# Layer 0 of an encoder kernel: eight output blocks over each x tile at the start, one first transfer, 25 warming products

## The chip, the cores and the metric

The kernel runs on one core of a Trainium2 chip. The metric is the device time of one execution in microseconds (us). Five engines matter: TensorE (PE, products), VectorE (DVE), ScalarE (ACT), GpSimd (POOL) and SyncE (SP, which issues most transfers).

## The reference

A trunk of two layers over 256 tokens and 1024 channels, float32, one batch. In each layer a normalised x goes through one large input projection; three mixers (a gated short convolution, a pooling mixer and windowed attention with grouped heads) are gated and added, and a SwiGLU follows:

```
h = rms_norm(x, g_mix)
proj = h @ w_in
b_a, c_a, x_a, u_p, q, k, v, ga, gp, gt = jnp.split(proj, split_points(), axis=-1)
y_a = short_conv_mixer(b_a, c_a, x_a, conv_w, w_a_out)
y_p = multiscale_pool_mixer(u_p, w_pool, pool_scale)
y_t = windowed_gqa(q, k, v, rel_bias, sink) @ w_attn_out
x = x + (sigmoid(ga) * y_a + sigmoid(gp) * y_p + sigmoid(gt) * y_t) @ w_o
gate, up = jnp.split(rms_norm(x, g_ffn) @ w_gu, [D_FF], axis=-1)
return x + (jax.nn.silu(gate) * up) @ w_down
```

## The kernel before

x lies transposed in SBUF: 128 channels on the partitions, eight x tiles (k = 0 to 7) of 256 tokens. Every matrix is cut into blocks of 128 x 128. All blocks lie in memory in the order in which they are used, which `plan_layer` writes out; 16 blocks make a chunk of 1 MB (`raw`), eight make a half chunk. A block's product is three matmuls of the float32r format (`mm3`, L161 to L165): the weights are split into `hi` and `lo` (`convert`, L136 on ACT and L137 on DVE), the activations likewise, and PE does hi x h (L163), hi x lo part of x (L164) and lo x h (L165). Below, "product" is one such matmul; a half chunk is 24 products.

`advance` keeps the conversions three half chunks ahead of PE. There are three `raw` buffers and five of `hi` and of `lo`, so a chunk's transfer waits until the third chunk before it is converted, and a conversion waits until PE is done with the fifth half chunk before it. The first two chunks arrive in pieces, with the x tiles between them (`dma_chunk`, L116 to L127), all issued by SP; the channel vectors `ch` (g_mix, g_ffn, the convolution's taps and the pooling scale) come first.

Normalisation is split. The first projections use `xg`, x times g_mix without the row factor (`xg_tiles`, L242: a pair h, lo for each x tile, h by DVE for the first two x tiles and by ACT after them, lo by DVE). Meanwhile `squares` sums the squares, `norm_stats` (L280) sums them over the partitions on PE (L283) and makes the reciprocal root `rr` through ACT (L285, then a table load) and a chain of small DVE steps, and `norm_rows` (L294) spreads it over the rows as `r` by four products (L299). What used `xg` is multiplied by `r` later. `make_h` makes the fully normalised pairs `h` for the later projections; it is issued after gate block MH.

Layer 0 starts with 21 products on a tile of zeros (`warm`, WARM = 21, L181). Then come K and V over each x tile in turn (`quad_outer`: four output blocks per x tile, 12 products), then the eight Q blocks one by one over all x tiles (`ntile`), with the sums (L283) after the first Q block, the rows (L299) and `kv_out` after the second, and the transposes of V (`vp`, L459) after the fourth. Eight gate blocks follow, then the convolution's blocks, with the attention's steps between them. PSUM has two pools of four banks, psA and psB.

A tile framework orders the instructions: a scheduler places the code's instructions on each engine's queue, and `issue_after` keeps a group behind one instruction. Each engine works through its queue in order.

Of the kernel before, what the change touches and what calls it, by code (L numbers as in the profile page):

```python
# [25 lines left out]
CB, CC, CX, CU, CQ, CK, CV, CGA, CGP, CGT = 0, 8, 16, 24, 32, 40, 42, 44, 52, 60  # L26
CT = 16
# [5 lines left out]
    HEADS += [4 * (2 * _p) + _g, 4 * (2 * _p + 1) + _g]  # L33


def plan_layer(last):

    out = []

    def inner(mat, ns, nk=KT):  # L40
        for n in ns:
            for k in range(nk):
                out.append((mat, k, n))

    def outer(mat, ns, nk=KT):
        for k in range(nk):
            for n in ns:
                out.append((mat, k, n))

    outer("in", (CK, CK + 1, CV, CV + 1))  # L50
    for q in range(2):
        inner("in", [CQ + 4 * q + j for j in range(4)])
    inner("in", [CGA + n for n in range(8)])
    for n in range(8):
        inner("in", (CC + n, CX + n, CB + n))
    inner("in", (CU, CU + 1))
    inner("a", range(8))
    for n in range(8):
        inner("in", (CGP + n, CGT + n))
        if n % 2 == 1 and n < 7:  # L60
            inner("in", (CU + n + 1, CU + n + 2))
        inner("t", (n,))
        out.extend(("pool", k, n) for k in range(2))
        if n >= 2:
            out.extend(("o", n - 2, m) for m in range(8))
    for j in range(4):
        out.extend(("o", k, m) for k in (6, 7) for m in (2 * j, 2 * j + 1))
    for q in range(NQ):
# [16 lines left out]


NCH = len(plan_layer(False)) * L // CT


@with_exitstack  # L90
def trunk(ctx, tc, wst, xT, chp, sinkb, rb, invc, gfin, ident_d, out):
    nc = tc.nc
    V, S, G, PE = nc.vector, nc.scalar, nc.gpsimd, nc.tensor

    const = ctx.enter_context(tc.tile_pool(name="const", bufs=1))
# [13 lines left out]

    plan = []  # L110
    for l in range(L):
        plan += [(l,) + key for key in plan_layer(l == L - 1)]
    raws, his, los = {}, {}, {}
    state = {"pos": 0, "dma": 0, "cv": 0}

    def dma_chunk(c):  # L116
        raw = wp.tile([P, CT * P], F32, name=f"raw{c}", tag="raw", bufs=3)
        if c < 2:
            if c == 0:
                nc.sync.dma_start(ch, chp)  # L120
            for a, b, xa, xb in (((0, 4, 0, 1), (4, 8, 1, 2), (8, 12, 2, 3), (12, 16, 3, 4)),
                                 ((0, 8, 4, 6), (8, 16, 6, 8)))[c]:
                nc.sync.dma_start(raw[:, a * P:b * P], wst[c, :, a * P:b * P])
                nc.sync.dma_start(x[:, xa:xb], xT[:, xa:xb])
# [54 lines left out]
    wps = psA.tile([P, 2 * T], F32, name="wps", tag="A")  # L179
    for _ in range(WARM):  # L180
        PE.matmul(wps[:, :T], warm[:, :P], warm, start=True, stop=True)  # L181
    x = act.tile([P, KT, T], F32, name="x")
    ch = const.tile([P, L, 6, KT], F32, name="ch")
    dma_chunk(0)
    dma_chunk(1)
    dma_chunk(2)
# [52 lines left out]
        return t[:, 0, :], t[:, 1, :]  # L239


    def xg_tiles(l, gi, j, st):  # L242

        for k in (2 * j, 2 * j + 1):
            g = ch[:, l, gi, k:k + 1]
            h, lo = pair(act, "xz", 8, "xg")
            if j < XJ:
                V.tensor_scalar(h, x[:, k], g, None, op0=ALU.mult)  # L248
            else:
                S.activation(h, x[:, k], AF.Copy, scale=g)  # L250
            V.scalar_tensor_tensor(lo, x[:, k], g, h.bitcast(F32), op0=ALU.mult, op1=ALU.subtract)  # L251
            st["xg"].append((h, lo))
# [41 lines left out]
    def norm_rows(st):  # L294

        rr, ps = st["q"], st["ps"]
        for i in range(4):
            tb = i % 2
            PE.matmul(ps[:, T:], rr[:, i:i + 1].to_broadcast([P, P]), ident2[:, P - tb * P:3 * P - tb * P],  # L299
                      start=(i == 0), stop=(i == 3))  # L300
# [21 lines left out]
    def newB(name="b"):  # L322
        return psB.tile([P, 2 * T], F32, name=nm(name), tag="B")
# [1 line left out]
    def newA(name="a"):  # L325
        return psA.tile([P, 2 * T], F32, name=nm(name), tag="A")

    def quad_outer(l, mat, ns, xs):
        banks = [newB(), newB()]
        for k in range(KT):  # L330
            for i, n in enumerate(ns):
                mm3(banks[i // 2][:, half(i % 2)], (l, mat, k, n), xs[k][0], xs[k][1],
                    start=(k == 0 and i % 2 == 0), stop=(k == KT - 1), skip=True)
        return banks

    def ntile(l, mat, n, xs, dst, nk=KT, koff=0):
        for k in range(nk):
            mm3(dst, (l, mat, k, n), xs[koff + k][0], xs[koff + k][1], start=(k == 0), stop=(k == nk - 1))
# [70 lines left out]
    def mixer(l, st):  # L409
        xg = st["xg"]  # L410
        def kv_out():
            norm_rows(st)
# [12 lines left out]
            for p in range(2):  # L425
                f = t1("vf")
                V.tensor_tensor(f[:, ::-1], vb[:, half(p)], r, op=ALU.mult)
                vf.append(f)
            return r, vf

        kb, vb = quad_outer(l, "in", (CK, CK + 1, CV, CV + 1), xg)
        ast = {"s": {}, "pt": {}, "ao": {}, "bias": {t: load_bias(t) for t in range(3)}}
        if l:
            norm_stats(st, AF.Exp)
        qs = []
        for qd in range(2):
            banks = [newB(), newB()]
            for i in range(4):
                ntile(l, "in", CQ + 4 * qd + i, xg, banks[i // 2][:, half(i % 2)])
                if l == 0 and qd == 0 and i == 0:  # L440
                    with tc.issue_after(last_mm[0].ins):
                        norm_stats(st, AF.Exp)
                if qd == 0 and i == 1 - l:
                    with tc.issue_after(last_mm[0].ins):
                        r, vf = kv_out()
# [9 lines left out]
            if qd == 0:  # L455
                for kt in range(2):
                    ps = newA("vp")
                    for p in range(2):
                        PE.transpose(ps[:, p * P:(p + 1) * P], vf[p][:, kt * P:(kt + 1) * P], ident)  # L459
                    vp = ps[:, :2 * P].rearrange("p (k j d) -> p k j d", k=2, j=2)  # L460
                    split(vt[kt][:, :, 0::3], vt[kt][:, :, 1:3], vp)
# [236 lines left out]
    st = {"xg": []}  # L698
    for j in range(4):
        convert(j)  # L700
        xg_tiles(0, 0, j, st)
    state["cv"] = 4
    for j in range(4):
        squares(j, st, V)
    with tc.issue_after(st["add"].ins):
        build_bias()
# [135 lines left out]
```

## Time and profile before

| | us |
|---|---|
| median of 3 runs | 980.25 (980.19 to 980.49) |
| the profiled execution | 981.37 |
| its span, first to last instruction | 979.6 |
| PE busy | 969.8 |
| DVE busy | 711.9 |
| ACT busy | 553.4 |

The profile is a record of one execution. Times on a timeline count from the span's start. A timeline row has the start, the duration, the engine, the line, the operation, what it writes and reads, the shape and how many instructions are merged in it; in brackets stands the idle time of the engine before it and what ended it. PE's durations overlap, so that PE's pace is read from the distance of the starts. A row of the waits has the total, the number and the longest. A row of the stretches has the stretch, its length, each engine's busy time with its instructions, the granted clock of PE, the share of time the DMA engines were busy, and GB/s.

### The profile page before, as it was taken

The numbers are of one execution on the slowest core, as the hardware profiler recorded it, in microseconds if no ns is written. First come the engines' busy times: TensorE is split into PE (matmuls) and PEld (weight loads), VectorE is DVE, ScalarE is ACT, GpSimd is POOL, SyncE is SP. The second block draws the span as 40 slices with busy tenths as digits, with TensorE's granted clock in tenths as the row PEclk, the third lists the DMA queues.
The fourth block names the chain that finished last, engine by engine and source line by source line (L and its number), as shares of the span: only waits on it lengthen the run. The fifth ranks groups of instructions, "written<-read, shape, count | busy, mean of one in ns | idle before, by whom it ended". The sixth has DMA issues, their size and how long they took to land.

```text
span 979.6 us, 19115 instructions
## 1 busy us (share of the span) xinstructions
PE 969.8 (99%) x7877; PEld 956.7 (98%) x7877; DVE 711.9 (73%) x1277; ACT 553.4 (56%) x916; POOL 41.4 (4%) x60
## 2 busy tenths in 40 slices
PE   8999999999999999999999999999999999999997
PEld 8999999999999999999999999999999999999996
DVE  7899888667668955546589888975777697555555
ACT  5866676654456544444577566765554574444443
POOL 6000000000002000000020000000000020000000
PEclk9999999999999999999999999999999999999999
DMA  8656544555554555455543745444554455545531
GB/s 299 230 192 207 184 162 160 194 177 193 183 201 171 179 181 200 179 178 195 188 173 130 248 160 181 143 170 173 185 203 173 172 194 178 209 173 188 197 132 43
DMA packets 27399, 178.11 MB, mean 182 GB/s; under 512 B 3312, under 2 KB 4096, under 8 KB 7088
## 3 DMA queue, kind: packets, MB, share of 16 engines
q1 hardware_dynamic: 25200, 169.93, 48.7%
q0 software_dynamic: 2112, 6.97, 2.5%
q8 instruction: 61, 1.00, 0.4%
q14 instruction: 26, 0.21, 0.1%
HBM read 175.80 MB, written 1.08 MB: 181 GB/s over the span
## 4 chain that ended last, share of the span: by engine, by line
PE 98%; DMA 1%; DVE 0%; ACT 0%; SPq 0%; issue 0%; DVEq 0%
PE b L164 25%; PE b L163 25%; PE b L165 25%; PE dn L165 2%; PE dn L163 2%; PE dn L164 2%; PE dn L623 2%; PE dn L622 2%; PE dn L621 2%; PE wo L163 2%; PE wo L164 2%; PE o L395 2%; PE wo L165 2%; PE pt L380 1%; PE sc L351 1%; PE sc L352 1%
## 5 line engine op out<-in xcount | busy, mean ns | idle before, releaser
L137 DVE TENSOR_TENSOR lo<-raw,hi 128x1024 fp32r<-128x1024 f32 (+1 forms) x322 | 390.0, 1219 | 208.8 <-ACT hi L136 208.3
L136 ACT ACTIVATE hi<-raw 128x1024 fp32r<-128x1024 f32 (+1 forms) x322 | 337.2, 1052 | 331.0 <-PE b L164 212.5
L163 PE MATMUL b<-h,hi 128*128 128x256 f32 x1344 | 379.8, 283 | 0.0
L165 PE MATMUL b<-h,lo 128*128 128x256 f32 x1344 | 378.4, 282 | 0.0
L164 PE MATMUL b<-h,hi 128*128 128x256 f32 x1344 | 378.3, 281 | 0.0
L164 PEld LDWEIGHTS b<-h,hi 128*128 128x128 f32 x1344 | 253.2, 188 | 0.2
L163 PEld LDWEIGHTS b<-h,hi 128*128 128x128 f32 x1344 | 253.2, 188 | 0.2
L165 PEld LDWEIGHTS b<-h,lo 128*128 128x128 f32 x1344 | 253.1, 188 | 0.0
L163 PE MATMUL b<-xg,hi 128*128 128x256 f32 x448 | 127.7, 286 | 1.2 <-DVE xg L248 1.2
L164 PE MATMUL b<-xg,hi 128*128 128x256 f32 x448 | 127.5, 285 | 0.2 <-DVE xg L251 0.2
L165 PE MATMUL b<-xg,lo 128*128 128x256 f32 x448 | 127.3, 284 | 0.0
L163 PEld LDWEIGHTS b<-xg,hi 128*128 128x128 f32 x448 | 85.6, 191 | 1.4 <-issue 1.4
L164 PEld LDWEIGHTS b<-xg,hi 128*128 128x128 f32 x448 | 85.7, 191 | 0.5 <-DVE xg L251 0.5
L165 PEld LDWEIGHTS b<-xg,lo 128*128 128x128 f32 x448 | 85.6, 191 | 0.0
L165 PE MATMUL dn<-fa,lo 128*128 128x256 f32 x176 | 49.5, 281 | 0.0
L164 PE MATMUL dn<-fa,hi 128*128 128x256 f32 x176 | 49.5, 281 | 0.0
L163 PE MATMUL dn<-fa,hi 128*128 128x256 f32 x176 | 49.5, 281 | 0.0
L364 ACT ACTIVATE s<-s,sm 128x256 f32<-128x256 f32 x64 | 31.8, 498 | 12.7 <-DVE sm L359 12.7
L163 PE MATMUL b<-z,hi 128*128 128x256 f32 x128 | 36.4, 284 | 0.0
L165 PE MATMUL b<-z,lo 128*128 128x256 f32 x128 | 36.1, 282 | 0.0
L165 PE MATMUL b<-ao,lo 128*128 128x256 f32 x128 | 36.0, 282 | 0.0
L163 PE MATMUL b<-ao,hi 128*128 128x256 f32 x128 | 36.0, 281 | 0.0
(176 smaller groups left out, 1496.6 us busy)
## 6 DMA issues: line engine op xcount, KB each, us to landing
raw<-wst SPq DMA_DIRECT2D x158, 1024.0 KB, 4.9
bias<-stab POOLq DMA_DIRECT2D x16, 384.0 KB, 4.2
raw<-wst SPq DMA_DIRECT2D x4, 256.0 KB, 5.5
raw<-wst SPq DMA_DIRECT2D x2, 512.0 KB, 6.2
out<-yg SPq DMA_DIRECT2D x4, 256.0 KB, 2.2
x<-xT SPq DMA_DIRECT2D x4, 128.0 KB, 5.4
x<-xT SPq DMA_DIRECT2D x2, 256.0 KB, 6.3
gf<-gfin POOLq DMA_DIRECT2D x2, 256.0 KB, 3.5
```

The source lines that it names most:

```text
L136: S.activation(hi[:, s], raw[:, s], AF.Copy)
L137: V.tensor_tensor(lo[:, s], raw[:, s], hi[:, s].bitcast(F32), op=ALU.subtract)
L163: PE.matmul(dst, wh, xh, start=start, stop=False, skip_group_check=skip)
L164: PE.matmul(dst, wh, xl, start=False, stop=False, skip_group_check=skip)
L165: last_mm[0] = PE.matmul(dst, wl, xh, start=False, stop=stop, skip_group_check=skip)
L351: PE.matmul(ps[:, half(j)], qs[t][j][:, cs], kh, start=True, stop=False)
L352: PE.matmul(ps[:, half(j)], qs[t][j][:, cs], kl, start=False, stop=True)
L364: S.activation(ss[i // 2][:, i % 2], ss[i // 2][:, i % 2], AF.Exp, bias=sm[:, 4 + i:5 + i], accum_out=sm[:, 12 + i:13 + i])
L395: PE.matmul(ps[:, half(j)], vv, pts[kt][i][:, half(j)], start=(kt == i == 0), stop=(kt == i == 1))
L621: PE.matmul(d, ah[:, cs], wh, start=(k == 0), stop=False)
L622: PE.matmul(d, ah[:, cs], wl, start=False, stop=False)
L623: PE.matmul(d, al[:, cs], wh, start=False, stop=(k == FT - 1))
```

## The change

- Layer 0 begins with K, V and the first four Q blocks over each x tile, eight blocks at a time (24 products per x tile instead of 12), into four PSUM banks, two of them of psA. The other four Q blocks follow one by one. The weights' order in memory follows.
- A function `arrive(k)` is called ahead of each x tile's products. It issues the pairs of x tiles 4 to 7 and the squares there (SQ), the sums (`norm_stats`) after x tile 5 and the rows (`norm_rows`) after x tile 6. `kv_out` comes after x tile 7, and the transposes of V after the last Q block.
- `ch` and x now lie in one tile and in one array in memory, and the channel vectors travel with x tile 0 in one first transfer. x tiles 2 and 3 come in one transfer as well.
- WARM is 25 instead of 21, and `make_h` is issued after gate 2 instead of gate 1 (MH).

```diff
-    outer("in", (CK, CK + 1, CV, CV + 1))
-    for q in range(2):
+    outer("in", (CK, CK + 1, CV, CV + 1) + (tuple(CQ + j for j in range(4)) if first else ()))
+    for q in range(int(first), 2):
         inner("in", [CQ + 4 * q + j for j in range(4)])
...
-            if c == 0:
-                nc.sync.dma_start(ch, chp)
-            for a, b, xa, xb in (((0, 4, 0, 1), (4, 8, 1, 2), (8, 12, 2, 3), (12, 16, 3, 4)),
+            for a, b, xa, xb in (((0, 4, 0, 1), (4, 8, 1, 2), (8, 12, 0, 0), (12, 16, 2, 4)),
                                  ((0, 8, 4, 6), (8, 16, 6, 8)))[c]:
+                s = slice(0 if xa == 0 else NG + xa * T, NG + xb * T)
+                if c == a == 0:
+                    nc.sync.dma_start(xc[:, s], xT[:, s])
                 nc.sync.dma_start(raw[:, a * P:b * P], wst[c, :, a * P:b * P])
-                nc.sync.dma_start(x[:, xa:xb], xT[:, xa:xb])
+                if xb > xa > 0:
+                    nc.sync.dma_start(xc[:, s], xT[:, s])
...
-    def quad_outer(l, mat, ns, xs):
-        banks = [newB(), newB()]
+    def quad_outer(l, mat, ns, xs, banks=None, before=None):
+        banks = banks or [newB(), newB()]
         for k in range(KT):
+            if before is not None:
+                before(k)
             for i, n in enumerate(ns):
...
-        kb, vb = quad_outer(l, "in", (CK, CK + 1, CV, CV + 1), xg)
+        ns = (CK, CK + 1, CV, CV + 1)
+        if l == 0:
+            kb, vb, *qbanks = quad_outer(l, "in", ns + tuple(CQ + j for j in range(4)), xg,
+                                         [newB(), newB(), newA("q"), newA("q")], arrive)
+            with tc.issue_after(last_mm[0].ins):
+                r, vf = kv_out()
+        else:
+            kb, vb = quad_outer(l, "in", ns, xg)
...
+    def arrive(k):
+
+        if k < 4:
+            xg_tiles(0, 0, 2 + k // 2, st, (4 + k,))
+        for j in SQ.get(k, ()):
+            squares(j, st, V)
+        if k == KT - 2:
+            with tc.issue_after(last_mm[0].ins):
+                norm_stats(st, AF.Exp)
+        if k == KT - 1:
+            with tc.issue_after(last_mm[0].ins):
+                norm_rows(st)
+            with tc.issue_after(st["add"].ins):
+                build_bias()
...
-WARM = 21
-MH = 1
+WARM = 25
+MH = 2
 XJ = 1
+
+SQ = {2: (0, 1), 4: (2,), 5: (3,)}
```

Line numbers of the changed kernel are three to twenty higher: L166 to L168 are the three products, L139 and L140 the conversions, L253 and L256 the pair, L290 the step behind the sums.

DVE's queue after its first clears, before: the pair of x tile 0 (`xg_160`) stands on both sides of the first `lo`.

```order
L248 TENSOR_SCALAR xg_160<-x,ch 128x256
L137 TENSOR_TENSOR lo_155<-raw_105,hi_154 128x512
L251 SCALAR_TENSOR_TENSOR xg_160<-x,ch,xg_160 128x256
L248 TENSOR_SCALAR xg_163<-x,ch 128x256
L137 TENSOR_TENSOR lo_155<-raw_105,hi_154 128x512
L251 SCALAR_TENSOR_TENSOR xg_163<-x,ch,xg_163 128x256
```

The same place now (`xg_161` is x tile 0, `xg_170` x tile 1):

```order
L253 TENSOR_SCALAR xg_161<-x 128x256
L256 SCALAR_TENSOR_TENSOR xg_161<-x,xg_161 128x256
L140 TENSOR_TENSOR lo_156<-raw_108,hi_155 128x512
L253 TENSOR_SCALAR xg_170<-x 128x256
L140 TENSOR_TENSOR lo_156<-raw_108,hi_155 128x512
L256 SCALAR_TENSOR_TENSOR xg_170<-x,xg_170 128x256
```

Both steps of x tile 0's pair now stand ahead of the first `lo`.

PE's queue where x tile 4 begins, before (`xg_175` is x tile 3, `xg_182` x tile 4; `b_232` and `b_233` are K's and V's banks): one product needing only hi is taken ahead.

```order
L164 MATMUL b_233<-xg_175,hi_166 128x256
L165 MATMUL b_233<-xg_175,lo_167 128x256
L163 MATMUL b_232<-xg_182,hi_178 128x256
L163 MATMUL b_233<-xg_182,hi_178 128x256
L164 MATMUL b_232<-xg_182,hi_178 128x256
L165 MATMUL b_232<-xg_182,lo_179 128x256
```

The same place now (`xg_191` is x tile 4, `q_189` and `q_190` are the Q banks, `hi_223` and `lo_224` the fifth half chunk):

```order
L168 MATMUL q_190<-xg_184,lo_181 128x256
L166 MATMUL b_187<-xg_191,hi_223 128x256
L167 MATMUL b_187<-xg_191,hi_223 128x256
L166 MATMUL b_188<-xg_191,hi_223 128x256
L167 MATMUL b_188<-xg_191,hi_223 128x256
L166 MATMUL q_189<-xg_191,hi_223 128x256
L167 MATMUL q_189<-xg_191,hi_223 128x256
L166 MATMUL q_190<-xg_191,hi_223 128x256
L168 MATMUL b_187<-xg_191,lo_224 128x256
```

Seven products that read hi alone now stand ahead of the first that reads lo.

ACT's queue around the step behind the sums (`nq`), before:

```order
L136 ACTIVATE hi_318<-raw_258 128x1024
L136 ACTIVATE hi_354<-raw_258 128x1024
L285 ACTIVATE nq_385<-ps_382,epst 128x2
L270 ACT_TABLE_LOAD
L270 ACTIVATE pre_388<-nq_385 128x1
L136 ACTIVATE hi_400<-raw_316 128x1024
```

and now (`raw_290` is the fifth chunk, as `raw_316` was):

```order
L139 ACTIVATE hi_292<-raw_221 128x1024
L139 ACTIVATE hi_323<-raw_221 128x1024
L139 ACTIVATE hi_358<-raw_290 128x1024
L139 ACTIVATE hi_402<-raw_290 128x1024
L290 ACTIVATE nq_389<-ps_386,epst 128x2
L275 ACT_TABLE_LOAD
L275 ACTIVATE pre_392<-nq_389 128x1
```

The fifth chunk's two conversions now stand ahead of `nq`.

More of the change, by code (lines that the diff above doesn't have):

```diff
@@ L33, with plan_layer @@
     HEADS += [4 * (2 * _p) + _g, 4 * (2 * _p + 1) + _g]
-def plan_layer(last):
+def plan_layer(last, first):
     out = []
@@ L84, in plan_layer, with trunk @@
     return out
-NCH = len(plan_layer(False)) * L // CT
+NCH = len(plan_layer(False, True)) * L // CT
+NG = L * 6 * KT
 @with_exitstack
-def trunk(ctx, tc, wst, xT, chp, sinkb, rb, invc, gfin, ident_d, out):
+def trunk(ctx, tc, wst, xT, sinkb, rb, invc, gfin, ident_d, out):
     nc = tc.nc
@@ L111, in trunk @@
     for l in range(L):
-        plan += [(l,) + key for key in plan_layer(l == L - 1)]
+        plan += [(l,) + key for key in plan_layer(l == L - 1, l == 0)]
     raws, his, los = {}, {}, {}
@@ L181, in trunk @@
         PE.matmul(wps[:, :T], warm[:, :P], warm, start=True, stop=True)
-    x = act.tile([P, KT, T], F32, name="x")
-    ch = const.tile([P, L, 6, KT], F32, name="ch")
+    xc = act.tile([P, NG + KT * T], F32, name="x")
+    ch = xc[:, :NG].rearrange("p (l g k) -> p l g k", l=L, g=6)
+    x = xc[:, NG:].rearrange("p (k t) -> p k t", k=KT)
     dma_chunk(0)
@@ L239, in pair, with xg_tiles @@
         return t[:, 0, :], t[:, 1, :]
-    def xg_tiles(l, gi, j, st):
-        for k in (2 * j, 2 * j + 1):
+    def xg_tiles(l, gi, j, st, ks=None):
+        for k in ks or (2 * j, 2 * j + 1):
             g = ch[:, l, gi, k:k + 1]
@@ L411, in kv_out @@
         def kv_out():
-            norm_rows(st)
+            if l:
+                norm_rows(st)
             r = st["r"]
@@ L436, in mixer @@
         for qd in range(2):
[L437 to L445, printed above, removed]
+            if l == 0 and qd == 0:
+                banks, nxt = qbanks, [newB(), newB()]
+                ntile(l, "in", CQ + 4, xg, nxt[0][:, half(0)])
+            elif l == 0:
+                banks = nxt
+                for i in range(1, 4):
+                    ntile(l, "in", CQ + 4 + i, xg, banks[i // 2][:, half(i % 2)])
+            else:
+                banks = [newB(), newB()]
+                for i in range(4):
+                    ntile(l, "in", CQ + 4 * qd + i, xg, banks[i // 2][:, half(i % 2)])
+                    if qd == 0 and i == 0:
+                        with tc.issue_after(last_mm[0].ins):
+                            r, vf = kv_out()
             for b in range(2):
@@ L454, in mixer @@
                     qs.append((qa, qb))
-            if qd == 0:
+            if qd == 1 - min(l, 1):
                 for kt in range(2):
@@ L700, in trunk @@
         convert(j)
-        xg_tiles(0, 0, j, st)
+        xg_tiles(0, 0, j // 2, st, (j,))
     state["cv"] = 4
[L703 to L706, printed above, removed]
+    def arrive(k):
[7 more added lines that the diff above has]
+        if k == KT - 1:
+            with tc.issue_after(last_mm[0].ins):
+                norm_rows(st)
+            with tc.issue_after(st["add"].ins):
+                build_bias()
     for l in range(L):
@@ L797 @@
     cols[4096:5120] = 4096 + perm
-    plans = [plan_layer(l == L - 1) for l in range(L)]
+    plans = [plan_layer(l == L - 1, l == 0) for l in range(L)]
     wst = np.empty((NCH, P, CT, P), a["w_in"].dtype)
@@ L818 @@
     wst = wst.reshape(NCH, P, CT * P)
-    xT = np.ascontiguousarray(a["x"][0].T.reshape(KT, P, T).transpose(1, 0, 2))
+    xT = a["x"][0].T.reshape(KT, P, T).transpose(1, 0, 2)
     chp = np.empty((P, L, 6, KT), a["g_mix"].dtype)
@@ L825 @@
             chp[:, l, i, :] = v.reshape(KT, P).T
+    xT = np.ascontiguousarray(np.concatenate([chp.reshape(P, NG), xT.reshape(P, KT * T)], axis=1))
     sinkb = np.ascontiguousarray(np.broadcast_to(a["attn_sink"][:, HEADS][None], (P, L, 16)))
@@ L829 @@
     invc = _constants()
-    arrays = {"wst": wst, "xT": xT, "chp": chp, "sinkb": sinkb, "rb": rb,
+    arrays = {"wst": wst, "xT": xT, "sinkb": sinkb, "rb": rb,
               "invc": invc, "gfin": gfin, "ident": np.eye(P, dtype=np.float32)}
@@ L837 @@
     with tile.TileContext(nc) as tc:
-        trunk(tc, aps["wst"], aps["xT"], aps["chp"], aps["sinkb"], aps["rb"],
+        trunk(tc, aps["wst"], aps["xT"], aps["sinkb"], aps["rb"],
               aps["invc"], aps["gfin"], aps["ident"], out)
```

## The prediction

> **What bounds the kernel now.** The table of busy times comes first, then the list of who waited for whom on TensorE (PE), then PE's timeline.
>
> ```profile
> PE 969.8 (99%) x7877; PEld 956.7 (98%) x7877; DVE 711.9 (73%) x1277; ACT 553.4 (56%) x916; POOL 41.4 (4%) x60
> PE wps L181 <- DVE epst L176: 1.2, 1, 1.2
> PE b L163 <- DVE xg L248: 1.2, 1, 1.2
> PE b L164 <- DVE xg L251: 0.2, 1, 0.2
> ```
>
> PE is busy for 99% of the span, and its three waits in the whole run all lie before 8.2 us. The one edit that counts products adds four warming ones, so the change can gain only at the start: an earlier first product, no holes behind it, or a better pace there. Everything later is a question of whether the other engines still keep ahead of a PE that comes sooner.
>
> ```profile
> 1.19 4.85 PE L181 MATMUL wps<-warm 128*128 128x256 f32 x21 [1.19 <-DVE epst L176]
> 7.21 0.76 PE L163 MATMUL b<-xg,hi 128*128 128x256 f32 x2 [1.17 <-DVE xg L248]
> 8.14 0.58 PE L164 MATMUL b<-xg,hi 128*128 128x256 f32 x1 [0.17 <-DVE xg L251]
> 8.53 0.41 PE L165 MATMUL b<-xg,lo 128*128 128x256 f32 x1
> 13.43 0.41 PE L165 MATMUL b<-xg,lo 128*128 128x256 f32 x1
> 13.64 0.32 PE L163 MATMUL b<-xg,hi 128*128 128x256 f32 x1
> 13.91 0.28 PE L165 MATMUL b<-xg,lo 128*128 128x256 f32 x1
> 24.59 0.28 PE L165 MATMUL b<-xg,lo 128*128 128x256 f32 x1
> 24.71 0.50 PE L283 MATMUL ps<-ones,s 128*128 128x1 f32 x4
> 25.08 0.36 PE L163 MATMUL b<-xg,hi 128*128 128x256 f32 x1
> 28.04 0.63 PE L299 MATMUL ps<-ident,rr 128*128 128x256 f32 x4
> 28.50 0.28 PE L163 MATMUL b<-xg,hi 128*128 128x256 f32 x1
> 34.20 0.60 PE L459 MATMUL vp<-ident,vf 128*128 128x128 f32 x4
> ```
>
> Start times show the pace. From 8.53 to 13.43 are 23 products, 0.213 us each; from 13.91 to 24.59 are 90 (30 blocks of three), 0.1187 us each. Before 13.64 every product, the 21 warming ones included, ran at half pace. 27 products were started by then, so 192 (the K, V and first Q quarter, 64 blocks) end at 13.64 + 165 x 0.1187 + 0.37 (the sums at L283) + 0.46 (the rows at L299) = 34.1; the trace has 34.20. **34.20 us is the mark**: the changed kernel also starts with 64 blocks and both norm steps, and from there PE's order is the same.
>
> What brought the full pace? 4.85 us of unbroken products (from 1.19) did not; the run that began at 8.14 did, after 5.50 us. I take it that an unbroken run of 4.9 to 5.5 us is needed, and that the hole of 1.17 us at 6.04 spoiled the first one. The table by stretches does not help, because its clock column (the last 1.00) reads full where the products are at half pace:
>
> ```profile
> 5.00:10.00 5.00, 3.66 (x15) 3.10 (x15) 3.29 (x8) 2.99 (x6) 2.94 (x5) 1.00 0.99 352
> ```
>
> **The change part by part.** First the feed of product 1.
>
> ```profile
> 0.74 0.39 SPq L120 DMA_DIRECT2D ch<-chp  x1
> 1.19 0.42 SPq L123 DMA_DIRECT2D raw<-wst  x1
> 1.66 0.42 SPq L124 DMA_DIRECT2D x<-xT  x1
> 5.02 0.63 ACT L136 ACTIVATE hi<-raw 128x512 fp32r<-128x512 f32 x1 [2.77 <-DMA raw<-wst]
> 6.71 0.35 DVE L248 TENSOR_SCALAR xg<-x,ch 128x256 fp32r<-128x256 f32 x1 [3.88 <-DMA x<-xT]
> 6.98 0.68 DVE L137 TENSOR_TENSOR lo<-raw,hi 128x512 fp32r<-128x512 f32 x1
> 7.50 0.63 ACT L136 ACTIVATE hi<-raw 128x512 fp32r<-128x512 f32 x1 [1.85 <-DMA raw<-wst]
> 7.58 0.51 DVE L251 SCALAR_TENSOR_TENSOR xg<-x,ch,xg 128x256 fp32r<-128x256 f32 x1
> ```
>
> Now the weights land at 5.02 and x tile 0 only at 6.71, and four VectorE (DVE) and ScalarE (ACT) steps follow. Afterwards x tile 0 goes out at 0.74 with the channel vectors, and the weights keep their slot at 1.19. They then land between 5.02 (same slot) and 6.71 (when the same three pieces have all landed today); I take 5.6, nearer to the row of the same slot. Then hi ends at 6.25 and lo at about 6.95 (0.63 + 0.68), with x tile 0's own pair long done.
>
> 25 warming products instead of 21 add 4 x 0.213 = 0.85 us: PE is busy until 6.04 + 0.85 = 6.9. They lie in a hole of 1.17 us, and would cost up to 0.6 only if the data were ready at 6.3. So product 1 starts at 6.9 and the third (the first that needs lo) at 6.95: no hole. An unbroken run from 1.19 reaches 5.5 us at 6.7, so I expect full pace from the first product on.
>
> At full pace 24 products per x tile last 2.85 us (12 lasted 1.42). Per x tile ACT has a conversion of 1.05, a pair member of 0.5 and half a square; DVE about 1.2 + 0.5 + 0.35: both under 2.85 but over 1.42, which is what eight blocks per tile buy. What holds PE next are two conversions:
>
> ```profile
> 11.46 1.06 ACT L136 ACTIVATE hi<-raw 128x1024 fp32r<-128x1024 f32 x1
> 12.55 1.23 DVE L137 TENSOR_TENSOR lo<-raw,hi 128x1024 fp32r<-128x1024 f32 x1 [0.35 <-ACT hi L136]
> 17.52 2.01 ACT L136 ACTIVATE hi<-raw 128x1024 fp32r<-128x1024 f32 x2 [1.09 <-DMA raw<-wst]
> 18.61 2.36 DVE L137 TENSOR_TENSOR lo<-raw,hi 128x1024 fp32r<-128x1024 f32 x2 [0.43 <-ACT hi L136]
> ```
>
> The first pair is the half chunk for x tile 2. ACT works back to back from 7.50 to it, on the same set of steps in both kernels, so it moves with the second weight piece (7.50 now, one SyncE slot of 0.46 earlier afterwards): lo is done between 13.3 and 13.78. PE wants it at 6.9 + 50 x 0.1187 = 12.85 and waits 0.5 to 0.9. The second pair belongs to x tile 4. Its 1 MB transfer is what ACT waited for (17.52); the bytes ahead of it are the same, so lo ends at 18.61 + 1.2 = 19.8 as now. The order puts seven products that need hi alone ahead of it, so PE reaches it after 103 products: 13.3 (or 13.78) + 53 x 0.1187 = 19.6 to 20.1. It goes on at 19.8 to 20.1.
>
> Left are 89 products, 10.56 us, and 0.37 + 0.46 for the norm steps: 31.2 to 31.5. My check sum above was 0.1 short, so 31.3 to 31.6 against 34.20: **2.6 to 2.9 us, taken as 2.8**. With neither wait it would be 6.9 + 192 x 0.1187 + 0.83 = 30.5, a gain of 3.7: the upper bound.
>
> The norm steps have moved into x tiles 6 and 7. PE has 29 products, 3.4 us, between them (3.0 now). The chain that must fit:
>
> ```profile
> 25.25 0.26 ACT L285 ACTIVATE nq<-ps,epst 128x2 f32<-128x2 f32 x1 [3.19 <-PE ps L283]
> 26.81 0.16 DVE L291 TENSOR_TENSOR rr<-nq,rr 128x2 fp32r<-128x2 f32 x1
> 26.94 1.99 ACT L136 ACTIVATE hi<-raw 128x1024 fp32r<-128x1024 f32 x2
> ```
>
> From the sums (24.71) to the end of rr (26.97) are 2.3 us; one lo of 1.2 now stands inside it on DVE: 3.5 against 0.3 + 3.4. It fits with 0.2 to spare and I charge nothing; without that cover it costs a few tenths. ACT's two conversions that follow nq today now stand ahead of it (third rival).
>
> Moving make_h one gate later (MH 2), and the K, V and Q work that now comes in one piece, cost nothing if DVE keeps its lead. Its tightest places today:
>
> ```profile
> 40.78 4.62 DVE L137 TENSOR_TENSOR lo<-raw,hi 128x1024 fp32r<-128x1024 f32 x4
> 58.47 1.22 DVE L137 TENSOR_TENSOR lo<-raw,hi 128x1024 fp32r<-128x1024 f32 x1
> ```
>
> The first of the four ends at 41.9, for a block that PE takes at 43.3; the one at 58.47 ends at 59.7 for 61.3. Afterwards the late one behind the K, V and Q work is the half chunk of gate 0. From r at about 30: two lo (2.3), kf and vf (4 x 0.36), then ACT's pace of 0.44 for 8 kk and 6 q halves, starting after a conversion that ends near 32.3: 38.4, plus a qf and the lo: 40.2. PE wants it at 31.4 + 4 x 2.85 + 0.35 = 43.2. Behind make_h the same sum leaves about 2 us. So no new stall. GpSimd's order is unchanged, and SyncE issues two transfers fewer, all weight pieces at their old slot or earlier.
>
> **Time.** The profiled execution took 981.37 (span 979.6 and 1.8 around it); minus 2.8 is 978.6. The median of the runs is 1.1 lower, 980.25; I take the gain from it: **977.5**.
>
> [...]
>
> **The rivals.**
>
> 1. *The clock stays at half: the change does not do what it says.* If the weights land near 6.71, lo ends at 8.1 and PE has holes at 6.9 to 7.4 and again before the third product; or products on a tile of zeros do not count. Then the unbroken run begins at 6.9 to 8.5 and the pace doubles at 12.4 to 14.0. Sum for 12.4: 26 products by then, 166 x 0.1187 + 0.83 gives 32.9; for 14.0: 33.7. Gain 0.5 to 1.2, time about **979.4**. For it: 4.85 us of warming did nothing; x tile 0 shows how late a third piece can be. Against it: the weights come second, and a run of 5.7 us is longer than the one that sufficed.
> 2. *The doubling falls at a different point from run to run.* Some executions before then had full pace by 8 us and were bound by DVE's pairs and the conversion ending at 19.8: the mark is near 31.9 there, and the gain on the median is 0.6 or so: **979.6**. Against it: the three runs lie within 0.3 us, where this would spread them by over 1. [...]
> 3. *The norm chain turns late: slower.* nq now queues behind two conversions of a 1 MB chunk, whose issue follows the lo that ends at 16.3. ACT is free for nq in time if the chunk lands by 23.2. Landings of such chunks:
>
> ```profile
> DMA to landing us min/median/max: 4.7/6.3/8.8
> ```
>
>    Median 22.6, longest 25.1: nq then ends 2 us late, with 1.8 lost. From a landing at 26.1 on, the wait eats the whole 2.8; with the bias tables on the same engines and a landing at 28.2, PE waits 5 us: **982.4**. Against it: it takes more than the longest landing.
> 4. *DVE becomes the bound between 40 and 65 us.* If the slack of about 2 us behind make_h or at gate 0 is overestimated by 4, PE loses 2: **979.4**. Against it: DVE had idle time before 30 us that moves into use.
>
> **How the numbers follow.** Forecast 0.60 (976.5 to 978.2), rival 1 0.16, rival 2 0.08, rival 3 0.05, rival 4 0.11. The range reaches from the gain without waits (980.25 - 3.7) to the middle of rivals 1 and 4: 976.5 to 979.6. A measurement of this kernel can tell about 0.2%, 2 us, from no change, so the border is 978.3: faster 0.62 (the forecast and a little of rivals 1 and 4), same 0.32, slower 0.06.
>
> **What would show it.** Right: starts 0.1187 us apart from the first product on (or by 10 us), PE waits of under 1 us at x tile 2 and next to none at x tile 4, the first product of the next Q block near 31.4, no PE wait later. Wrong: starts 0.213 us apart past 11 us (rival 1); a PE wait on rr or on the norm rows (rival 3); PE waits on lo after 40 us (rival 4).

## The result, and the profile after

| | before | after |
|---|---|---|
| median of 4 runs each, us | 980.22 (980.01 to 980.49) | 987.06 (986.51 to 987.32) |
| ratio of the times | | 1.0069, 95% interval 1.0051 to 1.0086 |
| profiled execution, us (its span) | 981.37 (979.6) | 987.1 (985.3) |

The changed kernel is 6.8 us slower, where 2.8 us less were forecast. Its page, table of busy times, and the list of who waited for whom on PE (us in total, times, longest):

```profile
PE 975.4 (99%) x7881; PEld 963.1 (98%) x7881; DVE 712.6 (72%) x1277; ACT 553.1 (56%) x916; POOL 37.2 (4%) x60
PE wps L184 <- DVE epst L179: 1.2, 1, 1.2
PE b L168 <- DVE lo L140: 0.8, 1, 0.8
PE q L168 <- DVE lo L140: 0.2, 1, 0.2
PE b L166 <- ACT hi L139: 0.2, 1, 0.2
```

PE is busy for 975.4 us instead of 969.8, with four products more, and waits no longer than before. So the time was not lost to a wait: PE itself takes longer for the same work. Where it does, its timeline shows. The start of after (start, duration, engine, line, output and inputs):

```profile
4.96 0.63 ACT L139 ACTIVATE hi<-raw 128x512 fp32r<-128x512 f32 x1 [2.72 <-DMA raw<-wst]
5.91 0.28 PE L166 MATMUL b<-xg,hi 128*128 128x256 f32 x1
6.03 0.28 PE L167 MATMUL b<-xg,hi 128*128 128x256 f32 x1
6.37 0.38 PE L168 MATMUL b<-xg,lo 128*128 128x256 f32 x1
14.41 0.39 PE L168 MATMUL b<-xg,lo 128*128 128x256 f32 x1 [0.76 <-DVE lo L140]
32.45 0.28 PE L166 MATMUL b<-xg,hi 128*128 128x256 f32 x1
68.38 0.28 PE L166 MATMUL b<-h,hi 128*128 128x256 f32 x1
977.55 0.39 PE L643 MATMUL dn<-hi,fa 128*128 128x512 f32 x1
```

and two rows of before for the last two:

```profile
69.74 0.28 PE L163 MATMUL b<-h,hi 128*128 128x256 f32 x1
971.90 0.39 PE L623 MATMUL dn<-hi,fa 128*128 128x512 f32 x1
```

The first product comes at 5.91 (7.21 before), at full pace. The mark, where the 192 first products are done, is at 32.45 instead of 34.20. At the first product of the first convolution block, after is still 1.36 us ahead (68.38 against 69.74). From there to the last product before took 902.16 us, after 909.17: **7.0 us are lost, on a stretch whose order of products is the same in both.**

The table by stretches says how. Its columns are the stretch, its length, PE's busy time and in brackets the number of its products, the clock, the DMA share and GB/s. One row of before:

```profile
320.00:480.00 160.00, 160.00 (x1351) 1.00 0.52 185
```

and the same stretch of after:

```profile
320.00:480.00 160.00, 160.00 (x1335) 1.00 0.52 184
```

No idle time and a full clock in both, but 16 products fewer: 160 us / 1351 = 118.4 ns, 160 / 1335 = 119.9 ns. (A count takes in two or three products that only reach into the stretch, so that these quotients read up to 0.3 ns low.) The start times in the trace give it more sharply. In before, the gaps from product to product in this stretch repeat a pattern between 115 and 122 ns whose mean is 118.7; in after every gap there is 120.0. The page's groups show the same in the weight load of the convolution blocks, here before (busy, mean ns of one):

```profile
L164 PEld LDWEIGHTS b<-h,hi 128*128 128x128 f32 x1344 | 253.2, 188 | 0.2
```

and after:

```profile
L167 PEld LDWEIGHTS b<-h,hi 128*128 128x128 f32 x1344 | 257.9, 192 | 0.2
```

The 512-wide products, from about 806 us on in before, in which the two operands change roles (the activations are loaded, hi and lo stream by), go the other way: 232.2 ns apart on average in before, 227.7 in after. That closes the account of the stretch, by start times: some 6600 gaps between 256-wide products with hi or lo grew by 1.1 to 1.4 ns, 8.0 us in all, and 254 gaps between 512-wide ones shrank by 4.5, 1.1 us.

Which edit can slow every product? None of those to the order. But the change takes the channel vectors (384 bytes per partition) out of the constants, which stand ahead of the buffers of the weights, and puts them into x's tile, behind these. So the buffers of raw, hi and lo stand 384 bytes lower than before, and all activations where they were. hi, lo and the activations repeat in steps that are multiples of 256 bytes, so one number describes all products with hi or lo: the **shift**, the address of an activation tile minus that of a weight buffer, modulo 256. The places that the two programs give: before 108768 - 45152 = 63616, a shift of 128; after 108768 - 44768 = 64000, a shift of 0. The sizes of what lies between the first hi buffer and the first pair of activations give the same: hi and lo 40960, x 8192, kk 8192, up 2176, vt 4096, in sum 63616, and after the change 384 more in x's tile. (The expectations below count the other way round, weights minus activations; a distance of 192 there is a shift of 64.)

### The profile page after: what moved, and what is told of

It reads as the page before. It is cut to its first block, busy times and chain, and to the rows that moved or that the text cites. A ratio compares the mean times of both kernels' runs of the same rounds, so it can differ in the third digit from the quotient of the medians.

```text
span 985.3 us, 19122 instructions
## 1 busy us (share of the span) xinstructions
PE 975.4 (99%) x7881; PEld 963.1 (98%) x7881; DVE 712.6 (72%) x1277; ACT 553.1 (56%) x916; POOL 37.2 (4%) x60
## 3 DMA queue, kind: packets, MB, share of 16 engines
q0 software_dynamic: 2112, 6.97, 2.4%
## 4 chain that ended last, share of the span: by engine, by line
PE 98%; DMA 1%; SPq 0%; ACT 0%; DVE 0%; issue 0%
PE b L166 25%; PE b L168 25%; PE b L167 25%; PE dn L168 2%; PE dn L167 2%; PE dn L166 2%; PE dn L642 2%; PE dn L641 2%; PE dn L643 2%; PE wo L166 2%; PE wo L167 2%; PE o L402 2%; PE wo L168 2%; PE pt L387 1%; DMA raw<-wst 1%; PE sc L359 1%
## 5 line engine op out<-in xcount | busy, mean ns | idle before, releaser
L140 DVE TENSOR_TENSOR lo<-raw,hi 128x1024 fp32r<-128x1024 f32 (+1 forms) x322 | 390.7, 1221 | 218.0 <-ACT hi L139 217.8
L139 ACT ACTIVATE hi<-raw 128x1024 fp32r<-128x1024 f32 (+1 forms) x322 | 337.1, 1053 | 337.1 <-PE b L167 212.7
L166 PE MATMUL b<-h,hi 128*128 128x256 f32 x1344 | 381.5, 284 | 0.0
L168 PE MATMUL b<-h,lo 128*128 128x256 f32 x1344 | 380.2, 283 | 0.0
L167 PEld LDWEIGHTS b<-h,hi 128*128 128x128 f32 x1344 | 257.9, 192 | 0.2
L166 PEld LDWEIGHTS b<-h,hi 128*128 128x128 f32 x1344 | 257.8, 192 | 0.2
L168 PEld LDWEIGHTS b<-h,lo 128*128 128x128 f32 x1344 | 257.8, 192 | 0.0
L168 PE MATMUL b<-xg,lo 128*128 128x256 f32 x416 | 117.7, 283 | 0.8 <-DVE lo L140 0.8
L166 PE MATMUL b<-xg,hi 128*128 128x256 f32 x416 | 118.2, 284 | 0.2 <-ACT hi L139 0.2
L167 PE MATMUL b<-xg,hi 128*128 128x256 f32 x416 | 117.6, 283 | 0.0
L168 PEld LDWEIGHTS b<-xg,lo 128*128 128x128 f32 x416 | 79.7, 192 | 1.2 <-DVE lo L140 1.2
L166 PEld LDWEIGHTS b<-xg,hi 128*128 128x128 f32 x416 | 79.8, 192 | 0.4 <-ACT hi L139 0.4
L167 PEld LDWEIGHTS b<-xg,hi 128*128 128x128 f32 x416 | 79.8, 192 | 0.0
L166 PE MATMUL dn<-fa,hi 128*128 128x256 f32 x176 | 49.8, 283 | 0.0
L168 PE MATMUL dn<-fa,lo 128*128 128x256 f32 x176 | 49.8, 283 | 0.0
L166 PE MATMUL b<-z,hi 128*128 128x256 f32 x128 | 36.5, 285 | 0.0
L166 PE MATMUL b<-ao,hi 128*128 128x256 f32 x128 | 36.2, 283 | 0.0
L167 PE MATMUL b<-ao,hi 128*128 128x256 f32 x128 | 36.2, 283 | 0.0
L168 PE MATMUL b<-ao,lo 128*128 128x256 f32 x128 | 36.2, 283 | 0.0
```

The costliest lines, as they stand in the source:

```text
L139: S.activation(hi[:, s], raw[:, s], AF.Copy)
L140: V.tensor_tensor(lo[:, s], raw[:, s], hi[:, s].bitcast(F32), op=ALU.subtract)
L166: PE.matmul(dst, wh, xh, start=start, stop=False, skip_group_check=skip)
L167: PE.matmul(dst, wh, xl, start=False, stop=False, skip_group_check=skip)
L168: last_mm[0] = PE.matmul(dst, wl, xh, start=False, stop=stop, skip_group_check=skip)
```

## The experiments

**Which part of the change is it?** Four kernels. e1 is after with the old places: 384 unused bytes back among the constants, 1664 behind x's tile (activations 2048 further, the shift of before).

```diff
     xc = act.tile([P, NG + KT * T], F32, name="x")
+    act.tile([P, 416], F32, name="pada")
+    const.tile([P, 96], F32, name="padc")
```

> The changed kernel with two unused tiles (384 bytes among the constants, 1664 bytes behind x), so that the weights hi and lo lie where they lay before and every activation tile lies where it lay plus 2048 bytes. Nothing else differs. The changed kernel's products start 120.0 ns apart for the whole run, those of the kernel before 118.7 ns on average. Places theory (the pace follows from where hi and lo lie in SBUF against the activations): starts 118.7 ns apart, 7150 x 1.3 ns = 9 us less than the changed kernel, so about 977.5 to 978.5. Start theory (the pace is set by what PE does when its clock is raised, amid warming products at 4.9 us): 120.0 ns and 987 as the changed kernel.

e2 is before with the channel vectors behind the weights, and thus the weights at after's place:

```diff
+    ch = act.tile([P, L, 6, KT], F32, name="ch")
     x = act.tile([P, KT, T], F32, name="x")
-    ch = const.tile([P, L, 6, KT], F32, name="ch")
```

> The kernel before with the channel vectors' tile moved from the constants to the place ahead of x, which moves hi and lo down by 384 bytes, to where the changed kernel has them, and leaves the activations where they are. Order and transfers are those of before. Places theory: 120.0 ns between starts, 980.2 + 9 = about 989.5. Start theory: unchanged, 980.2 within 0.5, 118.7 ns.

e3 is after with the old number of warming products (`WARM = 25` to `WARM = 21`), e4 is before with the new one (`WARM = 21` to `WARM = 25`).

> The changed kernel with 21 warming products instead of 25. Places theory: 120.0 ns stays, 986.5 to 988. Start theory: if the clock is raised later, amid real products as before, 118.7 ns, about 978 to 980; if it still rises amid warming products, 987.

> The kernel before with 25 warming products instead of 21. Places theory: 118.7 ns stays; the hole ahead of the first product shrinks from 1.2 to 0.3 us, so 978.5 to 980.3. Start theory: the clock rises amid warming products and the pace is 120.0 ns, 987 to 989.

| | shift | products in 320 to 480 us | median us | ratio to before (95%) |
|---|---|---|---|---|
| e1, after, old places | 128 | 1350 | 979.41 | 0.9994 (0.9985 to 1.0004) |
| e2, before, new places | 0 | 1336 | 987.52 | 1.0075 (1.0058 to 1.0092) |
| e3, after, 21 warming | 0 | 1336 | 986.49 | 1.0068 (1.0052 to 1.0083) |
| e4, before, 25 warming | 128 | 1350 | 979.23 | 0.9996 (0.9987 to 1.0005) |

The whole loss goes with the place: before's order gets it (e2), after's order loses it (e1). The four warming products change nothing that these medians can tell from noise, in either order. The 512-wide products follow the shift as well: 232.2 ns in e1, 227.8 in e2.

**The weights' own place, or the shift?** e5 keeps after's weights where they are and moves the activations by 128 bytes; e6 puts weights and activations back up by 384 bytes together; e7 and e8 move the activations by 256 and 384. For e5, e7, e8 (`[P, 32]`, `[P, 64]`, `[P, 96]`):

```diff
     xc = act.tile([P, NG + KT * T], F32, name="x")
+    act.tile([P, 32], F32, name="pada")
```

and for e6:

```diff
+    const.tile([P, 96], F32, name="padc")
```

> The changed kernel with an unused tile of 128 bytes behind x: hi and lo stay where the changed kernel has them, all activation operands of PE move up by 128 bytes, so that the distance from hi to them is what it was before, modulo 512 (384). Distance theory: starts 118.7 ns apart, 978.8 to 980. Own-place theory (what counts is where hi and lo lie themselves): 120.0 ns, 986 to 988.

> The changed kernel with 384 unused bytes among the constants: hi and lo lie exactly where they lay before, the activations 384 bytes higher, so that the distance modulo 512 stays that of the changed kernel (0). Distance theory: 120.0 ns, 986 to 988. Own-place theory: 118.7 ns, 978.8 to 980.

> The changed kernel with 256 unused bytes behind x (distance 256 modulo 512). Distance theory: a pace of its own, not known ahead; if only the distance 0 collides, 118.7 ns and 978.8 to 980. Own-place theory: 120.0 ns, 986 to 988.

> The changed kernel with 384 unused bytes behind x (distance 128 modulo 512). Distance theory: as for the gap of 256, 118.7 ns and 978.8 to 980 if only the distance 0 collides. Own-place theory: 120.0 ns, 986 to 988.

| | shift | products in 320 to 480 us | median us | ratio to before (95%) |
|---|---|---|---|---|
| e5 | 128 | 1350 | 979.23 | 1.0000 (0.9988 to 1.0011) |
| e6 | 0 | 1336 | 987.07 | 1.0071 (1.0048 to 1.0094) |
| e7 | 0 | 1335 | 986.28 | 1.0064 (1.0041 to 1.0086) |
| e8 | 128 | 1351 | 979.83 | 0.9994 (0.9982 to 1.0005) |

Weights at after's place with the old shift are as fast as before (e5), weights at before's place with shift 0 as slow as after (e6). So it is the shift, and 256 bytes more change nothing (e7). "Only multiples of 256 are slow" was then the simplest rule.

**What do other shifts give?** The same edit with tiles of 64, 192, 32, 224, 160 and 96 bytes, and e12, before with 64 bytes behind its x tile, which gives it e10's shift:

```diff
     x = act.tile([P, KT, T], F32, name="x")
+    act.tile([P, 16], F32, name="pada")
```

> The changed kernel with an unused tile of 64 bytes behind the x tile: the split weights stand 192 bytes (modulo 256) ahead of the activations. So far a distance of 0 gave 120.0 ns from product to product and 128 gave 118.7. If only the multiples of 256 are slow: 118.7 ns, about 979.3 us. If the pace goes with how far apart the two are: something between 118.7 and 120.0, 980 to 986 us. If 128 is itself only a second-best place: below 118.7, under 978 us.

> The same with 192 bytes: a distance of 64 (modulo 256). If only multiples of 256 are slow: 118.7 ns and about 979.3 us. If the pace goes with the distance in either direction: the same as with 192. If the order of the two matters too: another pace than with 192.

> The same with 32 bytes: a distance of 224 (modulo 256), the nearest to a multiple of 256 tried. If only multiples of 256 are slow: 118.7 ns and about 979.3 us. If what is slow is a band around them: 120.0 ns and about 986.5 us, or a value between.

> The kernel before, in its own order, with an unused tile of 64 bytes behind the x tile, which brings the weights to the distance of e10 (64 bytes, modulo 256). If the distance alone sets the pace: about 116 ns from product to product and 961 to 963 us. If e10's gain needs the new order as well: near 980 us.

> The changed kernel with 224 bytes behind the x tile: a distance of 32 (modulo 256). If the pace goes with how far apart the two are in either direction: as e11 (distance 224), 116.9 ns and about 967 us. If their order matters: another pace, as e9 and e10 differ; between 114 and 118 ns, 945 to 975 us.

> The same with 160 bytes: a distance of 96. Between its neighbours 64 (115.9 ns) and 128 (118.7 ns) if the pace changes smoothly: about 117.3 ns, 970 us. If each distance has a pace of its own: anything from 113.4 ns (the faster of e10's two paces, held all through: about 942 us) to 120.0.

> The same with 96 bytes: a distance of 160. Smooth between 128 (118.7 ns) and 192 (117.2 ns): about 118 ns, 975 us. If each distance has a pace of its own: anything from 113.4 to 120.0 ns.

| | shift | products in 320 to 480 us | median us | ratio to before (95%) |
|---|---|---|---|---|
| e11 | 32 | 1374 | 966.86 | 0.9876 (0.9860 to 0.9893) |
| e9 | 64 | 1361 | 969.85 | 0.9905 (0.9891 to 0.9920) |
| e15 | 96 | 1336 | 988.56 | 1.0093 (1.0077 to 1.0109) |
| e14 | 160 | 1366 | 972.50 | 0.9931 (0.9915 to 0.9946) |
| **e10** | **192** | **1414** | **961.11** | **0.9812 (0.9797 to 0.9826)** |
| e12, before's order | 192 | 1361 | 965.54 (959.78 to 966.27) | 0.9840 (0.9805 to 0.9875) |
| e13 | 224 | 1355 | 977.23 | 0.9975 (0.9965 to 0.9984) |

The simple rule falls, and so does every smooth one: 96 is as slow as 0, and before's 128 was itself a slow shift. **e10 beats both kernels: 1.9% under before, for 192 unused bytes.** e12 shows that it does not need the new order: one of its four runs took 959.78, the others 965.4 to 966.3.

Why e12 has two times, e10's own table by stretches suggests:

```profile
190.00:290.00 100.00, 100.00 (x851) 1.00 0.54 189
320.00:480.00 160.00, 160.00 (x1414) 1.00 0.54 191
```

100 us / 851 = 117.5 ns, 160 / 1414 = 113.2 ns: two paces in one run, at the same shift and the same clock. The change from the one to the other stands in PE's timeline of e10 (the dots stand for rows left out, the last ones for 175 us at the faster pace):

```profile
311.77 0.28 PE L167 MATMUL b<-xg,hi 128*128 128x256 f32 x1
311.89 0.28 PE L168 MATMUL b<-xg,lo 128*128 128x256 f32 x1
312.01 0.28 PE L166 MATMUL b<-xg,hi 128*128 128x256 f32 x1
...
312.86 0.74 PE L305 MATMUL ps<-ident,rr 128*128 128x256 f32 x4
313.44 0.28 PE L167 MATMUL b<-xg,hi 128*128 128x256 f32 x1
...
314.60 0.28 PE L168 MATMUL b<-xg,lo 128*128 128x256 f32 x1
314.71 0.28 PE L166 MATMUL b<-xg,hi 128*128 128x256 f32 x1
314.82 0.28 PE L167 MATMUL b<-xg,hi 128*128 128x256 f32 x1
314.94 0.28 PE L168 MATMUL b<-xg,lo 128*128 128x256 f32 x1
...
489.70 0.28 PE L168 MATMUL b<-xg,lo 128*128 128x256 f32 x1
489.81 0.50 PE L289 MATMUL ps<-ones,s 128*128 128x1 f32 x4
490.18 0.36 PE L166 MATMUL b<-xg,hi 128*128 128x256 f32 x1
490.73 0.28 PE L167 MATMUL b<-xg,hi 128*128 128x256 f32 x1
490.85 0.28 PE L168 MATMUL b<-xg,lo 128*128 128x256 f32 x1
490.96 0.28 PE L166 MATMUL b<-xg,hi 128*128 128x256 f32 x1
```

Starts are 0.12 apart until four products of another kind (L305) come between, and 0.11 soon after; that pace holds for some 175 us, until the next four of another kind (L289), and then it is 0.12 again. So a shift allows more than one steady pace, and an interruption can set a new one. e12's trace (of a longer run, 966.27) shows the same two paces:

```profile
320.00:480.00 160.00, 160.00 (x1361) 1.00 0.53 186
510.00:532.00 22.00, 22.00 (x196) 1.00 0.41 144
```

By start times these are 117.8 and 113.3 ns. From 312 to 495 us e12 has 1555 products in one go at 117.8, and e10 the same products at 113.3: 1555 x 4.44 ns = 6.9 us. e12's short run lies 6.5 us under the traced one. It left no trace, so that it had the faster pace in this stretch is likely and not shown.

**Does it need the other engines?** The shift also moves what ACT and DVE write against what PE reads. e16 measures the pace by itself: 2112 more products of zeros ahead of the kernel's own, from one tile with weights and moving operand in it, the second shifted by 16 bytes every 64 products. It ran once (1235.01 us).

```diff
+    ruler = const.tile([P, 444], F32R, name="ruler")
+    V.memset(ruler.bitcast(F32), 0.0)
...
+    for d in [0] + list(range(16)) + list(range(15, -1, -1)):
+        for _ in range(64):
+            PE.matmul(wps[:, :T], ruler[:, :P], ruler[:, P + 4 * d:P + 4 * d + T], start=True, stop=True)
```

> The changed kernel with 2112 extra products of zeros behind the warming ones: one static tile holds the weights and, behind them, the moving operand, shifted by 16 bytes every 64 products (0 twice, up to 240, and back down), while nothing converts weights or activations after the first microseconds. If TensorE's own two reads collide: the pace follows the shift as the gap did in the whole kernel: 120.0 ns at a shift of 0, 116.9 at 32, 117.8 or 113.4 at 64, 120.0 at 96, 118.7 at 128, 117.3 at 160, 113.4 or 117.8 at 192, 118.3 at 224. If the other engines' reads and writes are what collides: one pace at all shifts. About 250 us of extra time in all, with no use beyond the measurement.

The table by stretches of e16 shows how alone PE is there (after PE and its weight load come DVE, ACT and POOL, then clock, DMA share and GB/s):

```profile
30.00:37.00 7.00, 7.00 (x62) 7.00 (x61) 0.00 (x0) 0.00 (x0) 0.00 (x0) 1.00 0.00 0
67.80:74.80 7.00, 7.00 (x64) 7.00 (x63) 0.00 (x0) 0.00 (x0) 0.00 (x0) 1.00 0.01 2
105.50:112.50 7.00, 7.00 (x64) 7.00 (x63) 0.00 (x0) 0.00 (x0) 0.00 (x0) 1.00 0.00 0
30.00:250.00 220.00, 220.00 (x1872) 220.00 (x1871) 0.00 (x0) 0.00 (x0) 0.00 (x0) 1.00 0.00 1
```

From 30 to 250 us no other engine works and next to nothing is transferred. Still the 7 us at 30 (shift 32), 67.8 (shift 112) and 105.5 (shift 192) hold 62, 64 and 64 products. Exact values come from the start of each shift's first product in the trace (at shift 0 the second 64 on the way up): the difference to the next shift's first start, divided by 64, going up and coming back down, in ns. Beside them stand 160 us over the products of the stretch from 320 to 480 us in the whole kernel (the changed kernel's order):

| shift | ruler up | ruler down | whole kernel |
|---|---|---|---|
| 0 | 120.0 | 120.0 | 119.9 (after) |
| 16 | 118.8 | 116.7 | |
| 32 | 116.7 | 116.8 | 116.4 (e11) |
| 48 | 118.3 | 118.3 | |
| 64 | 117.8 | 117.8 | 117.6 (e9) |
| 80 | 119.8 | 118.3 | |
| 96 | 119.9 | 120.0 | 119.8 (e15) |
| 112 | 113.7 | 113.9 | 119.9 (e17) |
| 128 | 118.6 | 118.7 | 118.5 (e5) |
| 144 | 118.7 | 118.6 | |
| 160 | 117.3 | 117.4 | 117.1 (e14) |
| 176 | 119.2 | 119.2 | |
| 192 | 113.6 | 113.8 | 113.2 (e10) |
| 208 | 119.2 | 119.2 | |
| 224 | 118.3 | 118.3 | 118.1 (e13) |
| 240 | 117.2 | 117.1 | |

At every shift that had been run in the whole kernel by then, PE alone gives the same pace to 0.6 ns (at 192 the faster one; e10's other stretch was at 117.5). So PE with its weights and its moving operand is enough for the effect (113.6 to 120.0 ns in the ruler); the other engines and the transfers are not needed. 16 and 80 differ on the way up and down: two paces there too.

**Does the best of the ruler hold?** The ruler's 113.7 to 113.9 at shift 112 (113.3 behind the first ten products) asked for a trial, in both orders: the split weights 16 bytes on in their buffers, and in after's order 128 bytes behind x.

```diff
-        hi = wp.tile([P, HT * P], F32R, name=f"hi{hc}", tag="hi", bufs=5)
-        lo = wp.tile([P, HT * P], F32R, name=f"lo{hc}", tag="lo", bufs=5)
+        hi = wp.tile([P, HT * P + 64], F32R, name=f"hi{hc}", tag="hi", bufs=5)[:, 4:4 + HT * P]
+        lo = wp.tile([P, HT * P + 64], F32R, name=f"lo{hc}", tag="lo", bufs=5)[:, 4:4 + HT * P]
```

> The changed kernel with the activations 128 bytes on and the split weights 16 bytes on in their buffers (made 256 bytes longer, so that each keeps the place): a shift of 112, which gave 113.3 ns in the ruler. If that pace holds all through: about 7150 products x (118.7 - 113.3) = 39 us under e5, near 941 us. If this distance has a second, slower phase after each interruption, as 64 bytes had in e10: 945 to 975 us.

> The kernel before with the split weights 16 bytes on in their buffers, which gives the same shift of 112. If the pace is the distance alone: 113.3 ns and about 941 us. If the change's order is worth what was forecast for it, 2.6 to 2.9 us more than e17; if it is worth only what e1 and e5 showed, 0.2 to 0.8 us more than e17.

It does not hold. e17 took 985.00 us (ratio 1.0055, 1.0041 to 1.0069) and e18 985.58 (1.0063, 1.0050 to 1.0076), both with 1335 products in the stretch from 320 to 480 us, 119.9 ns. e17's start times show three paces by turns: 116.7 ns from 14 to 24 us, 118.3 from 700 to 780, 120.0 from 420 to 480, and hardly any of the 113.3. Here the weights moved by 16 bytes, in the ruler the moving operand; whether that matters, or only which of its paces a run falls into, was not told apart.

## Why the prediction was wrong

**The step that failed: "34.20 us is the mark: the changed kernel also starts with 64 blocks and both norm steps, and from there PE's order is the same."** The order is the same; the time of its products is not. The sum took 0.1187 us per product from before, and kept it for a kernel whose weights stand elsewhere. No term of the sum and no rival was about a place in memory, though the diff shows that the channel vectors leave the constants. That cost 7.0 us in the profiled executions, and nothing in the range allowed for it. Where the shift is that of before the sum comes near: e1's profiled execution (979.00) is 2.4 us under before's (981.37), for a forecast of 2.6 to 2.9 from that profile.

**A second step had the wrong size: "The median of the runs is 1.1 lower, 980.25; I take the gain from it."** The gain was worked out from a profiled execution of before whose pace doubled late, at 13.64; the median stands for executions in which it did so earlier. e4 shows this, before's own order with four more warming products:

```profile
8.07 0.27 PE L165 MATMUL b<-xg,lo 128*128 128x256 f32 x1
8.18 0.28 PE L163 MATMUL b<-xg,hi 128*128 128x256 f32 x1
31.92 0.60 PE L459 MATMUL vp<-ident,vf 128*128 128x128 f32 x4
```

Full pace by 8.1, mark at 31.92. In e1, the changed order at the same shift, the mark is at 31.95:

```profile
31.95 0.28 PE L166 MATMUL b<-xg,hi 128*128 128x256 f32 x1
```

So once the pace is full early, the new order adds nothing at the mark, and e4's median is 0.8 us under before's in the same runs (979.23 against 980.03; the ratio's interval holds 1). Behind the mark the profiled executions of before, e1 and e4 take the same time (947.05 to 947.17 us), so an execution of before at the median, 980.22, would have its mark near 33.1, not at 34.20. e2, whose start has before's order and 21 warming products, has it there (33.11), and shows how the point of doubling moves:

```profile
1.19 4.45 PE L181 MATMUL wps<-warm 128*128 128x256 f32 x21 [1.19 <-DVE epst L176]
8.05 0.28 PE L165 MATMUL b<-xg,lo 128*128 128x256 f32 x1
8.17 0.28 PE L163 MATMUL b<-xg,hi 128*128 128x256 f32 x1
8.62 0.42 PE L164 MATMUL b<-xg,hi 128*128 128x256 f32 x1
8.84 0.42 PE L165 MATMUL b<-xg,lo 128*128 128x256 f32 x1
11.82 0.28 PE L164 MATMUL b<-xg,hi 128*128 128x256 f32 x1
11.94 0.28 PE L165 MATMUL b<-xg,lo 128*128 128x256 f32 x1
33.11 0.60 PE L459 MATMUL vp<-ident,vf 128*128 128x128 f32 x4
```

Full pace already among the last warming products (21 in 4.45 us instead of 4.85), half from 8.41, full again from 11.82. Between the warming products and 8.41 PE had waited 1.7 (1.25 ahead of 6.90 and 0.46 ahead of 7.83). With the same 21 products e18 goes the same way (half pace from 9.01 to 12.42), e12 has full pace from its first own product at 6.83 on, and the profiled run of before had half pace until 13.64. What sets the point was not shown.

This is rival 2 in kind, and its gain on the median, 0.6, is what e1 gives (979.41 against 980.03); it had a chance of 0.08. Against it the prediction held that three runs lay within 0.3 us, where it would spread them by over 1. The 64 runs of before that were taken beside the experiments lie between 978.81 and 981.97; the 26 with a mean granted clock of 0.996 (e2's profiled run has that too) have a median of 980.16, the other 38 (0.997 to 0.999) one of 979.5. Three runs were too few to see that.

The other steps, by their own words:

- *What bounds the kernel*: right. PE is busy for 99% in all of these kernels, and the PE waits that came up later in some of them stay under 1 us in sum; so DVE does not become the bound (rival 4), and the norm rows cost PE no wait (rival 3).
- *"I expect full pace from the first product on"*: right in this execution, for a reason that does not hold; rival 1 was wrong. The prediction took an unbroken run of 4.9 to 5.5 us to be needed. In after the 25 warming products took 4.88 us, hardly more than 21 did before (4.85):

```profile
1.19 4.88 PE L184 MATMUL wps<-warm 128*128 128x256 f32 x25 [1.19 <-DVE epst L179]
```

  Their starts are 0.213 us apart up to 4.77 and 0.12 from 4.96 on: the pace doubled after some 3.7 us of products, and in e1 only near 6.8, behind its first own product at 6.70. That, and weights earlier than forecast (hi at 4.96, under the lower bound of 5.02), put the first product at 5.91 instead of 6.9.
- *The wait at x tile 2*: right in kind, 0.8 us where 0.5 to 0.9 were given. But PE goes on there at 14.41, not at 13.3 to 13.8, and this, with 142 products at 120.0 instead of 118.7 behind it (0.2 us), puts the mark at 32.45 instead of 31.3 to 31.6. The row of the conversion behind it, in after:

```profile
12.04 1.06 ACT L139 ACTIVATE hi<-raw 128x1024 fp32r<-128x1024 f32 x1 [0.88 <-DMA raw<-wst]
13.13 1.22 DVE L140 TENSOR_TENSOR lo<-raw,hi 128x1024 fp32r<-128x1024 f32 x1 [1.23 <-ACT hi L139]
```

  ACT had nothing left to do and waited 0.88 us for the half chunk itself; the prediction had it work back to back to this conversion, as before, and charged no transfer there.
- *No wait at x tile 4*: right.

At equal shift, then, the order that the change sets up is worth next to nothing: e1, e5 and e8 against before (shift 128) 0.9994, 1.0000 and 0.9994; after against e2 (shift 0) 987.06 to 987.52; e17 against e18 (shift 112) 985.00 to 985.58. None of these differences is over 0.1%. At shift 192, e10 is 4.4 us under e12, but the pace of one long stretch accounts for more than that (6.9 us in the traces), and one run of e12 is as fast as e10's.

## What to carry to other kernels

Before a change is costed by its order of work, look at what it allocates: a tile taken from or added to the memory ahead of a kernel's main operands moves these against each other, and here, with PE busy for 99%, 1.1% of its pace (120.0 ns for 118.7) took 7.0 us where the repair at the start had brought 1.4. Compare the start-to-start time of the main product in both profiles first (products per long stretch without idle time); if it differs, pad a few bytes and time again, here in steps of 32, before any other theory. And take a gain at the start from an execution that stands for the median, not from a profile that lies outside the timed runs.

## What the runs showed of the hardware

- A product of 128x256 with its own weight load took from 113.3 to 120.0 ns, start to start, by the shift between weights and moving operand modulo 256 bytes (256 bytes more: 986.28 us in e7 beside 987.06 in after, 979.83 in e8 beside 979.23 in e5). It did so with PE alone at work (113.6 to 120.0 ns in e16) and in the whole kernel: 961.1 to 988.6 us for the same instructions. The 512-wide products had other paces at the same shifts: 227.7 ns at 0, 229.0 (e10) at 192, 232.2 at 128, on average.
- One shift can have several steady paces (113.3 and 117.8 at 192; 116.7, 118.3 and 120.0 at 112). In e10 one was kept for 175 us in which nothing came between, and an interruption changed it. What decides which one follows, and how the pace comes from the two addresses, stays open.
- Other engines are not needed for the effect. In e16, from 30 to 250 us, DVE, ACT and POOL have no instruction and the DMA share is 0.00; there only the address of the moving operand against that of the weights changes, and the pace with it (113.6 to 120.0 ns).
